# A first MLP whose weight sums are made in device memory during the attention, with two plain groups instead of three

## The chip, the cores and the metric

The kernel runs on one core of a Trainium2 chip. A core has a matrix engine (TensorE, "PE" in the profile), a vector engine (VectorE, "DVE"), an activation engine (ScalarE, "ACT"), a general engine (GpSimd, "POOL"), and a queue engine (SyncE, "SP") that issues loads. Sixteen DMA engines move data between device memory and the core's on-chip memory (SBUF). Plain loads are issued by SP and form queue 1 (hardware_dynamic); a DMA that adds to its destination is issued by POOL and forms queue 0 (software_dynamic). Each engine runs its instructions in order, and waits on semaphores where an operand or a buffer is not ready. TensorE accumulates into eight banks of PSUM. The metric is the device time of the whole program in microseconds (us).

## The reference, cut to what matters

The program is a two-layer decoder trunk on 512 tokens of width 1024, all in float32. Layer 0 is attention and an MLP, layer 1 a gated short convolution and an MLP.

```python
h = x
h = h + attention_mixer(h, ...)       # 8 softmax heads, 8 stick-breaking heads, one output projection
h = h + conv_ffn(h, ...)              # the "first MLP"
h = h + short_conv_mixer(h, ...)
h = h + conv_ffn(h, ...)

def conv_ffn(h, norm_g, w_up, conv_w, w_down):      # D_FF = 2816
    xn = rms_norm(h, norm_g)
    u = causal_dwconv(xn @ w_up, conv_w)            # w_up: 1024 x 5632
    g, val = u[..., :D_FF], u[..., D_FF:]
    return (jax.nn.silu(g) * val) @ w_down
```

The change concerns `xn @ w_up` of the first MLP.

## The kernel before

**Precision.** Every float32 operand of a product is split into a high and a low half (ScalarE copies the high half, VectorE subtracts it to give the low one), and each product is three matmuls: high x high, high x low, low x high. So each weight tile of 128 x 1024 costs a DMA, one ScalarE copy (`whi`) and one VectorE subtraction (`wlo`).

**Plain weights.** `want` lists weight tiles in the order of use; `weights()` hands out the next and at once emits the load and split of the tile two further on (`fetch`, `load`, `split_all`; SP issues at L256, the splits are L262 and L263). Loaded tiles live in a ring of three buffers with the tag `raw`, the halves in rings of three `whi` and three `wlo`. SP runs ahead of the other engines: a load is issued as soon as the split three tiles before it has freed a `raw` buffer. The attention's query and key weights are loaded as 128 columns at a time, rows of 512 bytes, 1024 rows a tile; its value weights as 256 columns, 512 rows of 1024 bytes.

**The attention.** Twenty-four units (head pair by query blocks) run in a software pipeline: `logits` of unit g, then `weigh` of an earlier one and `turn` (transposes) of unit g-1, with projections as fillers between (`fill`). ScalarE takes exponentials and sigmoids out of the score banks and copies the high halves out of the transposes; it also does the weight splits, in the same queue. POOL does little there: some constants, a memset of `fwide` (L494), and small memsets of the `rest` tile in the stick-breaking heads (L687, L690).

**The first MLP's up projection.** The output columns are handled in 11 groups of 256 gate and 256 value columns (`HF` = 11). A *plain* group (0, 1 and 2; `CLASSIC = 3`) is four blocks of 128 columns; each block is 8 x 3 matmuls of 512 columns into one bank (`products`, L283 to L285). The other groups, *seven groups*, use a block scheme with seven products in place of eight (`Sevens`): the tokens are split in two halves of 256, the 1024 inputs in two halves of 512, and the columns into gate and value. Each product (`seven`, L1011) is 24 matmuls of 256 columns. Products are called p1, p7, p3, p6, p2, q5, q4, one per *slot*, and each has a weight operand and a token operand (a "form", made once by `prepare` from the normalised residual). With X, Y, W, Z for the four 512 x 256 weight blocks (first inputs gate, first inputs value, last inputs gate, last inputs value), the weight operands are: p1: X; p2: W; p3: Z; p7: Y + Z; p6: Y + Z + X; q4: Y + Z + X + W; q5: X + Y. Before, Y is loaded by SP, the Z block is added by an accumulating DMA from POOL (`add_block`), and VectorE then adds X (L1063) and W (L1111) in place; Y is added onto X by another accumulating DMA.

**Order.** The program is written to a planner that orders each engine's instructions by its own estimate of readiness. An instruction wrapped in `pin` (or `keep_in_program_order`) stays behind what was written before it on its engine; this sets an order and no wait for any other engine. Work of VectorE and ScalarE that is not urgent (normalising plain groups' outputs, preparing forms, the convolution and gate of plain groups) is written as generators in a list of *chores*, each step with a nominal cost; `work_off(us)` runs that much of it. It is called per matmul triple in plain blocks with `SHARE` = 0.58, and per slot in the first seven group.

**Banks.** Tags a, b and c have 2, 4 and 2 of the eight banks. A plain block's accumulator is freed when its `normed` chore has read it.

**The convolution stage** uses the same class `Sevens` with `ahead = True`; its p6 weights are split in slot 1, after a copy of the first product's bank to another bank (L1102) on ScalarE.

Of the kernel before, what the change touches and what calls it, by code (L numbers as in the profile page):

```python
# [25 lines left out]
P = 128  # L26
S = 512
# [26 lines left out]
def trunk(  # L54
# [384 lines left out]
    def want_conv_out():  # L439
        for o in range(ND):  # L440
            want(conv_w_out[0], 0, 8, o * P, P)
        want_ffn(1, 2 * CLASSIC)

    want_ffn(0, 2 * CLASSIC)

    def products(acc, w, order=tuple(range(ND))):
        for k in order:
# [188 lines left out]
    def logits(p, u):  # L636
# [33 lines left out]
        if fox:  # L670
            m = len(bs)
            top, total, inv = (tiny.tile([P, m, 2], F32, tag=f"{t}{m}", name=f"{t}{p}{u}") for t in ("top", "total", "inv"))
            for j, (b, n, c, a) in enumerate(parts):
                for e in range(2):
                    dve.reduce_max(top[:, j, e:e + 1], ss[e][:, c:c + n], axis=AX.X, negate=True)
                    act.activation(own[j][:, e, :], ss[e][:, c:c + n], AF.Exp, bias=top[:, j, e:e + 1], accum_out=total[:, j, e:e + 1])
            for es in at_once(u):
                dve.reciprocal(inv[:, :, es], total[:, :, es])
                for j in range(m):
                    for e in range(es.start, es.stop):  # L680
                        dve.tensor_scalar(own[j][:, e, :], own[j][:, e, :], inv[:, j, e:e + 1], None, op0=ALU.mult)
        else:

            scale = q_scale[p]
            if not rests:
                rests.append(aw.tile([P, 2, S + 1], F32, tag="rest", name="rest", bufs=1))
                pool.memset(rests[0][:, :, S:S + 1], 0.0)  # L687
# [328 lines left out]
    class Sevens:  # L1016

        def __init__(self, name, mp, groups, block_of):
            self.name, self.mp, self.groups, self.block_of = name, mp, groups, block_of
            self.forms = {n: [mp.tile([P, 4, HT], F32R, tag=f"{n}_{i}", name=f"{n}_{i}{name}") for i in ("hi", "lo")] for n in FORMS}  # L1020
            self.st, self.wides = {}, {}
# [7 lines left out]
        def load_one(self, g, n, kh, half):  # L1029
            t = self.st[g][n] = wp.tile([P, CHUNK], F32, tag="raw", name=f"{n}{self.name}{g}")[:, 0:1024].rearrange("p (k c) -> p k c", c=2 * P)  # L1030
            nc.sync.dma_start(t, self.block_of(g, kh, half))
# [28 lines left out]

        def first_sums(self, g):
            self.weights_of(g, "p7", "Y")
            dve.tensor_tensor(self.st[g]["Y"], self.st[g]["Y"], self.st[g]["X"], op=ALU.add)  # L1063
# [11 lines left out]
        def slot(self, g, s):  # L1075

            on, was, soon = (i in self.groups for i in (g, g - 1, g + 1))
            if g == self.groups[0]:
                self.work_off(1.4 if s < 4 else 1e9)
            form, n, fresh = (("p1", "A", True), ("p7", "T", True), ("p3", "R", False), ("p6", "R", False), ("p2", "A", False),  # L1080
                              ("q5", "R", False), ("q4", "T", False))[s]
            if s == 2:
# [5 lines left out]
            if s == 0:  # L1088
# [2 lines left out]
                        self.weights_of(p, "p3", "Z")  # L1091
                    self.join(p, "yg", st[p]["T"], st[p]["Xs"])
                if on:
                    self.load_one(g, "W", 1, 0)
                if soon:
                    self.load_pair(g + 1)
            elif s == 1:
                first = not was and not self.ahead
                if on and first:
                    self.weights_of(g, "p6", "Y")  # L1100
                if on:
                    act.activation(self.bank_of(g, "R"), c["A"], AF.Copy, scale=-1.0)  # L1102
                if on and not first:
                    self.weights_of(g, "p6", "Y")
                if soon:
                    self.add_block(g + 1, "Y", 1, 1)
            elif s == 2:
                if on:
                    self.kept(g, "P7s", c["T"])
                    self.weights_of(g, "p2", "W")  # L1110
                    dve.tensor_tensor(c["Y"], c["Y"], c["W"], op=ALU.add)  # L1111
            elif s == 3:
                if was:
                    self.early(p, st[p]["R"])
                if on:
                    self.weights_of(g, "q5", "X")
            elif s == 4:
                if on:
                    self.kept(g, "Xs", c["R"])
                    self.weights_of(g, "q4", "Y")  # L1120
            if was and s != 2:
                self.tail(p, s)
            if s == 5:
                if on:
                    self.load_one(g, "Z", 1, 1)
                    self.open_wides(g)
                    self.left(g, c["A"])
                if soon:
# [7 lines left out]
                    self.first_sums(g + 1)  # L1136

        chores, credit, ahead = (), 0.0, False

        def work_off(self, us):  # L1140
            if self.norm.row is None:
# [9 lines left out]
    def up_seven(layer, norm, mp):  # L1151

        blocks = Blocks(mp, layer)
        w_up, base = ffn_w_up[layer], CLASSIC
# [5 lines left out]
        up = Sevens(layer, mp, range(CLASSIC, HF), block_of)  # L1160
        up.norm, up.chores = norm, []
        up.wides_of = lambda g: {n: mp.tile([P, 2, S], F32, tag=n, name=f"{n}{layer}{g}", bufs=1) for n in ("yg", "yv", "ug", "uv")}
        wides, forms, chores = up.wides, up.forms, up.chores

        def taps_of(g, half, i):
# [49 lines left out]
            blocks.product(2 * g + i, 1, u[0][:, i:i + 1, :], u[1][:, i:i + 1, :])  # L1215
            yield 0.86

        for j in range(2 * CLASSIC):
            accs = []
            for half in range(2):  # L1220
                accs.append(bank("ab"[half]))
                for _ in products(accs[-1], weights()):
                    up.work_off(SHARE)
                if j == 2 * CLASSIC - 1 and half == 1:
                    up.weights_of(base, "p1", "X")
                    up.first_sums(base)
            if j == 2 * CLASSIC - 2:
                up.load_pair(base)
                up.add_block(base, "Y", 1, 1)
# [5 lines left out]
        slots = [(lambda g=g, s=s: up.slot(g, s)) for g in range(CLASSIC, HF + 1) for s in range(7)]  # L1235
        return blocks, slots

    def conv_seven(norm, mp):
# [109 lines left out]
        for j in range(8):  # L1348
# [26 lines left out]
    def mlp(layer, norm, mp):  # L1375
# [60 lines left out]
                else:  # L1436
                    pin(dve.tensor_tensor(b, b, d, op=ALU.add))

        n_up = 7 * (HF - CLASSIC)
        for i, fn in enumerate(slots[:n_up]):  # L1440
            fn()
            left = n_up - i
# [177 lines left out]
```

## Time and profile before

| what | value |
|---|---|
| median of 3 runs | 1133.82 us (1133.34 to 1135.28) |
| profiled execution | 1133.66 us |
| its span, first to last instruction | 1131.9 us |
| TensorE busy | 1120.0 us, 99% |
| VectorE busy | 965.3 us, 85% |
| ScalarE busy | 670.5 us, 59% |
| queue 1 (plain loads) | 106.94 MB, 30.7% of 16 DMA engines |
| queue 0 (issued by POOL) | 47.10 MB, 25.0% |

In the profile a group of instructions is named by its line, its engine, its operation and its tiles (`out<-in`). "Busy" of TensorE counts pipelined matmuls whose ends are modelled. In a timeline the first column is the start and the second the duration in us, and the brackets hold how long the engine was idle before, and what ended that. A DMA view gives for each queue its packets, megabytes and the time its packets took as a share of sixteen engines over the stretch. By time, the attention runs from about 40 to 275 us, the first MLP's up projection from 280 to 513 us (plain groups until 347 us), its down projection to about 620 us, the convolution stage from there to about 760 us, and then comes the second MLP.

### The profile page before, as it was taken

Reading aid. Unit: us, or ns where it says so; the run is one execution under the profiler, and the core shown is the slowest. Engines: PE = TensorE matmul, PEld = TensorE weight load, DVE = VectorE, ACT = ScalarE, POOL = GpSimd, SP = SyncE. Lnnn points to the kernel's source line nnn. Section 1 sums busy time; section 2 is a strip of 40 time slices with the busy share of each in tenths; the row PEclk is TensorE's granted clock in tenths of the full one; section 3 lists DMA queues with packets and bytes.
Section 4 is the critical chain, followed back from the end, with each engine's and each line's share of the span. In section 5 each row is a group of like instructions: output and inputs, shape, how many; then the busy total and the mean of one; then the engine's idle time right before and its main releaser. Section 6 shows DMA issues by size and latency. Waiting matters only on the chain.

```text
span 1131.9 us, 19049 instructions
## 1 busy us (share of the span) xinstructions
PE 1120.0 (99%) x7547; PEld 1005.0 (89%) x7547; DVE 965.3 (85%) x1459; ACT 670.5 (59%) x999; POOL 133.0 (12%) x150
## 2 busy tenths in 40 slices
PE   8999999999999999999999999999999999999998
PEld 6888787878889999999999889988889999998886
DVE  5787888887899899989989889875798899989886
ACT  7556676655455766666557455543445767667554
POOL 4000000000002111014400001000002111014300
PEclk9999999999999999999999999999999999999999
DMA  6412212032375877789963455533375876789961
GB/s 193 113 38 75 57 38 75 21 93 75 94 195 113 182 176 152 178 222 216 227 179 77 115 152 132 124 112 93 94 195 112 176 184 146 177 224 220 228 160 56
DMA packets 160440, 155.31 MB, mean 137 GB/s; under 512 B 6396, under 2 KB 136492, under 8 KB 160352
## 3 DMA queue, kind: packets, MB, share of 16 engines
q1 hardware_dynamic: 124256, 106.94, 30.7%
q0 software_dynamic: 35936, 47.10, 25.0%
q8 instruction: 59, 0.97, 0.4%
q14 instruction: 29, 0.24, 0.1%
q10 hardware_dynamic: 160, 0.07, 0.0%
HBM read 149.10 MB, written 2.10 MB: 134 GB/s over the span
## 4 chain that ended last, share of the span: by engine, by line
PE 90%; DVE 5%; ACT 2%; DMA 1%; issue 1%; SPq 0%; DVEq 0%; ACTq 0%
PE psb L1011 24%; PE psb L1532 11%; PE psa L1011 10%; PE psa L1532 8%; PE psb L283 6%; PE psb L285 6%; PE psb L284 6%; PE psa L285 4%; PE psa L284 4%; PE psa L283 4%; PE psb L658 1%; PE psa L754 1%; DVE rest L699 1%; DVE wlo L263 1%; DMA X<-in_ffn_w_up 1%; PE psc L730 1%
## 5 line engine op out<-in xcount | busy, mean ns | idle before, releaser
L262 ACT ACTIVATE whi<-raw 128x1024 fp32r<-128x1024 f32 (+2 forms) x97 | 100.1, 1033 | 97.3 <-PE psa L284 29.2
L263 DVE TENSOR_TENSOR wlo<-raw,whi 128x1024 fp32r<-128x1024 f32 (+2 forms) x97 | 115.3, 1190 | 26.0 <-ACT whi L262 25.1
L1011 PE MATMUL psb<-p_lo,whi_p 128*128 128x256 f32 x384 | 108.1, 281 | 0.0
L1011 PE MATMUL psb<-p_hi,wlo_p 128*128 128x256 f32 x384 | 108.1, 281 | 0.0
L1011 PE MATMUL psb<-p_hi,whi_p 128*128 128x256 f32 x384 | 107.8, 281 | 0.0
L283 PE MATMUL psb<-hs_a,whi 128*128 128x512 f32 x256 | 104.8, 409 | 0.0
L285 PE MATMUL psb<-hs_a,wlo 128*128 128x512 f32 x256 | 101.4, 397 | 0.0
L1011 PEld LDWEIGHTS psb<-p_hi,whi_p 128*128 128x128 f32 x384 | 72.8, 190 | 0.0
L1011 PEld LDWEIGHTS psb<-p_lo,whi_p 128*128 128x128 f32 x384 | 72.3, 188 | 0.0
L1011 PE MATMUL psb<-q_hi,whi_q 128*128 128x256 f32 x256 | 72.1, 282 | 0.2 <-ACT Xs L1059 0.2
L1011 PE MATMUL psa<-p_hi,wlo_p 128*128 128x256 f32 x256 | 72.2, 282 | 0.0
L1011 PEld LDWEIGHTS psb<-p_hi,wlo_p 128*128 128x128 f32 x384 | 72.2, 188 | 0.0
L1011 PE MATMUL psb<-q_hi,wlo_q 128*128 128x256 f32 x256 | 72.1, 282 | 0.0
L1011 PE MATMUL psb<-q_lo,whi_q 128*128 128x256 f32 x256 | 72.0, 281 | 0.0
L1011 PE MATMUL psa<-p_lo,whi_p 128*128 128x256 f32 x256 | 72.0, 281 | 0.0
L1011 PE MATMUL psa<-p_hi,whi_p 128*128 128x256 f32 x256 | 71.8, 281 | 0.0
L1532 PE MATMUL psb<-act,whi 128*128 128x256 f32 x352 | 63.0, 282 | 0.1
L393 DVE SCALAR_TENSOR_TENSOR uv<-yv,taps,uv 128x511 f32<-128x511 f32 (+1 forms) x88 | 62.9, 745 | 0.2
L393 DVE SCALAR_TENSOR_TENSOR ug<-yg,taps,ug 128x511 f32<-128x511 f32 (+1 forms) x88 | 62.1, 745 | 0.3 <-ACT ug L390 0.3
L285 PEld LDWEIGHTS psb<-hs_a,wlo 128*128 128x128 f32 x256 | 48.1, 188 | 11.2 <-DVE wlo L263 0.2
L283 PEld LDWEIGHTS psb<-hs_a,whi 128*128 128x128 f32 x256 | 48.4, 189 | 10.5 <-issue 1.2
L1532 PE MATMUL psb<-whi,act 128*128 128x512 f32 x176 | 56.5, 398 | 0.0
(458 smaller groups left out, 3643.4 us busy)
## 6 DMA issues: line engine op xcount, KB each, us to landing
raw<-in_attn_w_in SPq DMA_DIRECT2D x24, 512.0 KB, 3.9
raw<-in_ffn_w_up SPq DMA_DIRECT2D x24, 512.0 KB, 3.8
X<-in_ffn_w_up SPq DMA_DIRECT2D x16, 512.0 KB, 4.7
W<-in_ffn_w_up SPq DMA_DIRECT2D x16, 512.0 KB, 6.8
Y<-in_ffn_w_up SPq DMA_DIRECT2D x16, 512.0 KB, 4.4
Z<-in_ffn_w_up SPq DMA_DIRECT2D x16, 512.0 KB, 4.7
Y<-in_ffn_w_up POOLq DMA_DIRECT2D x16, 512.0 KB, 9.8
X<-in_ffn_w_up POOLq DMA_DIRECT2D x16, 512.0 KB, 7.5
```

Of the source, the lines that this page charges most:

```text
L262: return (act.activation(hi[:, at_], raw[:, at_], AF.Copy), dve.tensor_tensor(lo[:, at_], raw[:, at_], f32(hi[:, at_]), op=ALU.subtract))
L263: dve.tensor_tensor(lo[:, at_], raw[:, at_], f32(hi[:, at_]), op=ALU.subtract))
L283: made = [pe.matmul(acc, w[0], rhs[0], start=first, stop=False), pe.matmul(acc, w[0], rhs[1], start=False, stop=False), pe.matmul(acc, w[1 ...
L284: pe.matmul(acc, w[0], rhs[1], start=False, stop=False),
L285: pe.matmul(acc, w[1], rhs[0], start=False, stop=last)]
L393: dve.scalar_tensor_tensor(dst[:, d:], src[:, 0:S - d], tap(j), dst[:, d:], op0=ALU.mult, op1=ALU.add)
L658: pe.matmul(ss[e][:, c:c + wide], ql[rows, b * P:n], kl[rows, 0:wide], start=first and b == bs[0], stop=last and b == bs[-1])
L699: dve.tensor_tensor_scan(back, back, begin[:, S - n:S][:, ::-1], 0.0, op0=ALU.mult, op1=ALU.max)
L730: pe.transpose(t[:, k * P:(k + 1) * P], w[:, e, k * P:(k + 1) * P], ident)
L754: pe.matmul(out_, w, t[:, first:first + step * (NB - k - 1) + 1:step, :], start=k == 0 and i == 0, stop=k == NB - 1 and i == 1)
L1011: pe.matmul(to, w[a][:, k, c], x[b][:, k, :], start=fresh and i + k + t == 0, stop=i == 1 and k == 3 and t == 2, skip_group_check=not fresh)
L1532: pe.matmul(to, l, r, start=begin and o + t == 0, stop=end and t == 2 and o == (0 if layer else 1), skip_group_check=not fresh)
```

## The change

Five things change: three belong to the first MLP, one to the attention, one to the convolution stage.

1. `PLAIN = 2, 3`: in the first MLP two plain groups, in the second still three. The plain blocks' banks become a, b / a, b / b, b / c, c. In the loop over plain blocks only group 0 is normalised and both halves of the forms prepared; group 0's gates and all of group 1 become chores that are worked off during the seven groups, 1.4 us a slot in the first and 0.5 us a slot after it. Group 1's wide tiles live in the space of `hs_a`.
2. `table_steps` makes three tables in device memory, for groups 2 to 10 in three chunks of three groups: "7" = Y + Z, "6" = that plus X, "4" = that plus W. It takes six steps of three DMAs, all on POOL's queue, each 512 rows of 768 floats: a copy, an accumulate, a copy of the made table, an accumulate, and again. They are handed out one by one, one before the attention's `fill(PRE)` and one per unit, each pinned behind POOL's last instruction.
3. In the first MLP's seven groups the sums are loaded as plain blocks: Y comes from table 7, two further loads bring "p6 sum" and "q4 sum" into the `raw` ring, and both VectorE additions and Y's accumulating DMA go. SP's loads of these groups are pinned. X's accumulating DMA stays.
4. The memsets of the stick-breaking `rest` tile move from POOL to VectorE.
5. In the convolution stage the p6 weights of its first group are split before the slots rather than in slot 1.

```diff
-CLASSIC = 3
+PLAIN = 2, 3
+CHUNKS = (2, 3), (5, 3), (8, 3)
...
+    far = ctx.enter_context(tc.tile_pool(name="far", bufs=1, space=bass.MemoryType.DRAM))
...
+    tables = {}
+
+    def table_steps():
+
+        w = ffn_w_up[0]
+        for n in "764":
+            for g, m in CHUNKS:
+                tables[n, g] = far.tile([512, m * 256 + 16], F32, tag=f"t{n}{g}", name=f"t{n}{g}")
+        def block(kh, half, g, m):
+            return w[kh * 512:(kh + 1) * 512, half * DFF + g * 256:half * DFF + (g + m) * 256]
+        for step in range(6):
+            n = "764"[step // 2]
+            for g, m in CHUNKS:
+                to = tables[n, g][:, 0:m * 256]
+                if step % 2:
+                    src = block(*((0, 1), (0, 0), (1, 0))[step // 2], g, m)
+                    pin(nc.gpsimd.dma_start(to, src, accum_op=ALU.add))
+                else:
+                    pin(nc.gpsimd.dma_start(to, block(1, 1, g, m) if step == 0 else tables["76"[step // 2 - 1], g][:, 0:m * 256]))
+                yield
+
+    def table_of(n, group):
+        g, m = next(c for c in CHUNKS if c[0] <= group < c[0] + c[1])
+        return tables[n, g][:, (group - g) * 256:(group - g + 1) * 256].rearrange("(k p) c -> p k c", p=P)
...
-                pool.memset(rests[0][:, :, S:S + 1], 0.0)
+                dve.memset(rests[0][:, :, S:S + 1], 0.0)
             rest = rests[0]
             if u == 0:
-                pool.memset(rest[:, :, P:P + 1], 0.0)
+                dve.memset(rest[:, :, P:P + 1], 0.0)
...
+    sums_far = table_steps()
+    next(sums_far)
     fill(PRE)
     for g in range(len(units) + 2):
+        next(sums_far, None)
...
-            nc.sync.dma_start(s["X"], self.block_of(g, 0, 0))
-            nc.sync.dma_start(s["Y"], self.block_of(g, 0, 1))
+            self.held(nc.sync.dma_start(s["X"], self.block_of(g, 0, 0)))
+            self.held(nc.sync.dma_start(s["Y"], self.table("7", g) if self.table else self.block_of(g, 0, 1)))
...
         def first_sums(self, g):
             self.weights_of(g, "p7", "Y")
-            dve.tensor_tensor(self.st[g]["Y"], self.st[g]["Y"], self.st[g]["X"], op=ALU.add)
+            if not self.table:
+                dve.tensor_tensor(self.st[g]["Y"], self.st[g]["Y"], self.st[g]["X"], op=ALU.add)
             self.add_block(g, "X", 0, 1)
+            if self.table:
+                self.load_one(g, "p6 sum", self.table("6", g))
...
-            if g == self.groups[0]:
-                self.work_off(1.4 if s < 4 else 1e9)
+            if self.chores:
+                self.work_off(self.rate(g, s))
...
-                first = not was and not self.ahead
-                if on and first:
-                    self.weights_of(g, "p6", "Y")
+                first = not was
+                if on and first and not self.ahead:
+                    self.weights_of(g, "p6", "p6 sum" if self.table else "Y")
...
-                if soon:
+                if soon and not self.table:
                     self.add_block(g + 1, "Y", 1, 1)
...
-                    dve.tensor_tensor(c["Y"], c["Y"], c["W"], op=ALU.add)
+                    if self.table:
+                        self.load_one(g, "q4 sum", self.table("4", g))
+                    else:
+                        dve.tensor_tensor(c["Y"], c["Y"], c["W"], op=ALU.add)
...
+        if layer == 0:
+            up.table = table_of
+            up.rate = lambda g, s: 1.4 if g == base else 0.5
...
+                accs.append(bank(("ab", "ab", "bb", "cc")[j][half] if layer == 0 else "ab"[half]))
...
+            if layer == 0:
+                if j < 2:
+                    chores.extend((normed(0, j, accs), prepare(j)))
+                continue
...
+        if layer == 0:
+            chores.extend([gate_one(0, i) for i in range(2)] + [normed(1, i, kept[2 + i]) for i in range(2)] + [gate_one(1, i) for i in range(2)])
...
                 up.first_sums(1)
+                up.weights_of(1, "p6", "Y")
         want_conv_out()
```

More of the change, by code (lines that the diff above doesn't have):

```diff
@@ L1020, in __init__ @@
             self.forms = {n: [mp.tile([P, 4, HT], F32R, tag=f"{n}_{i}", name=f"{n}_{i}{name}") for i in ("hi", "lo")] for n in FORMS}
-            self.st, self.wides = {}, {}
+            self.st, self.wides, self.table = {}, {}, None
         def load_pair(self, g):
@@ L1025, in load_pair, with held, load_one @@
             s["X"], s["Y"] = (self.mp.tile([P, 4, 2 * P], F32, tag=t, name=f"{t}{self.name}{g}", bufs=2) for t in "XY")
-            nc.sync.dma_start(s["X"], self.block_of(g, 0, 0))
-            nc.sync.dma_start(s["Y"], self.block_of(g, 0, 1))
-        def load_one(self, g, n, kh, half):
+            self.held(nc.sync.dma_start(s["X"], self.block_of(g, 0, 0)))
+            self.held(nc.sync.dma_start(s["Y"], self.table("7", g) if self.table else self.block_of(g, 0, 1)))
+        def held(self, made):
+            if self.table:
+                pin(made)
+        def load_one(self, g, n, src):
             t = self.st[g][n] = wp.tile([P, CHUNK], F32, tag="raw", name=f"{n}{self.name}{g}")[:, 0:1024].rearrange("p (k c) -> p k c", c=2 * P)
-            nc.sync.dma_start(t, self.block_of(g, kh, half))
+            self.held(nc.sync.dma_start(t, src))
         def add_block(self, g, n, kh, half):
@@ L1103, in slot @@
                 if on and not first:
-                    self.weights_of(g, "p6", "Y")
-                if soon:
+                    self.weights_of(g, "p6", "p6 sum" if self.table else "Y")
+                if soon and not self.table:
                     self.add_block(g + 1, "Y", 1, 1)
@@ L1119, in slot @@
                     self.kept(g, "Xs", c["R"])
-                    self.weights_of(g, "q4", "Y")
+                    self.weights_of(g, "q4", "q4 sum" if self.table else "Y")
             if was and s != 2:
@@ L1138, in trunk, with rate @@
         chores, credit, ahead = (), 0.0, False
+        def rate(self, g, s):
+            return 1.4 if s < 4 else 1e9
         def work_off(self, us):
@@ L1158, in block_of, with wides_of @@
             return w_up[kh * 512:(kh + 1) * 512, c0:c0 + 2 * P].rearrange("(k p) c -> p k c", p=P)
-        up = Sevens(layer, mp, range(CLASSIC, HF), block_of)
+        up = Sevens(layer, mp, range(base, HF), block_of)
         up.norm, up.chores = norm, []
-        up.wides_of = lambda g: {n: mp.tile([P, 2, S], F32, tag=n, name=f"{n}{layer}{g}", bufs=1) for n in ("yg", "yv", "ug", "uv")}
+        if layer == 0:
+            up.table = table_of
+            up.rate = lambda g, s: 1.4 if g == base else 0.5
+        def wides_of(g):
+            if layer == 0 and g == base - 1:
+                t = hsp.tile([P, 8, S], F32, tag="hs_a", name=f"hs_a_wide{layer}")
+                return {n: t[:, 2 * i:2 * i + 2, :] for i, n in enumerate(("yg", "yv", "ug", "uv"))}
+            return {n: mp.tile([P, 2, S], F32, tag=n, name=f"{n}{layer}{g}", bufs=1) for n in ("yg", "yv", "ug", "uv")}
+        up.wides_of = wides_of
         wides, forms, chores = up.wides, up.forms, up.chores
@@ L1216, in gate_one @@
             yield 0.86
-        for j in range(2 * CLASSIC):
+        kept = []
+        for j in range(2 * base):
             accs = []
             for half in range(2):
-                accs.append(bank("ab"[half]))
+                accs.append(bank(("ab", "ab", "bb", "cc")[j][half] if layer == 0 else "ab"[half]))
                 for _ in products(accs[-1], weights()):
                     up.work_off(SHARE)
-                if j == 2 * CLASSIC - 1 and half == 1:
+                if j == 2 * base - 1 and half == 1:
                     up.weights_of(base, "p1", "X")
                     up.first_sums(base)
-            if j == 2 * CLASSIC - 2:
+            if j == 2 * base - 2:
                 up.load_pair(base)
-                up.add_block(base, "Y", 1, 1)
+                if not up.table:
+                    up.add_block(base, "Y", 1, 1)
+            kept.append(accs)
+            if layer == 0:
+                if j < 2:
+                    chores.extend((normed(0, j, accs), prepare(j)))
+                continue
             chores.append(normed(j // 2, j % 2, accs))
@@ L1234, in up_seven @@
                 chores.append(gate_one(i // 2, i % 2))
-        slots = [(lambda g=g, s=s: up.slot(g, s)) for g in range(CLASSIC, HF + 1) for s in range(7)]
+        if layer == 0:
+            chores.extend([gate_one(0, i) for i in range(2)] + [normed(1, i, kept[2 + i]) for i in range(2)] + [gate_one(1, i) for i in range(2)])
+        slots = [(lambda g=g, s=s: up.slot(g, s)) for g in range(base, HF + 1) for s in range(7)]
         return blocks, slots
```

13 lines of the change are left out of this document (7 added, 6 removed).

## The prediction

> **What bounds the kernel now.** I read the page first, then the busy times by stretch, then the waits by engine, and last the DMA queues and the order of the loads in the attention. From the page come the span, the engines, and TensorE, granted clock and DMA in 40 slices of 28.3 us:
>
> ```profile
> span 1131.9 us, 19049 instructions
> PE 1120.0 (99%) x7547; PEld 1005.0 (89%) x7547; DVE 965.3 (85%) x1459; ACT 670.5 (59%) x999; POOL 133.0 (12%) x150
> PE   8999999999999999999999999999999999999998
> PEclk9999999999999999999999999999999999999999
> DMA  6412212032375877789963455533375876789961
> ```
>
> TensorE is busy 1120.0 of 1131.9 us at full clock: time is won by giving it less to do, and lost wherever it is made to wait. The DMA engines are mostly idle in slices 3 to 11 (the attention) and busy in the MLP. The profiled execution took 1133.66 us, 1.8 us around its span and 0.16 under the median 1133.82; I sum against 1133.7.
>
> The next rows are two stretches: the last plain group of the first MLP, four blocks of 24 matmuls, then one group of seven products (the columns are length, busy time and count of PE, PEld, DVE, ACT, POOL, then clock, DMA share and GB/s).
>
> ```profile
> 324.61:346.97 22.36, 22.36 (x98) 18.06 (x96) 21.59 (x34) 10.76 (x16) 2.49 (x2) 1.00 0.61 156
> 367.52:387.41 19.89, 19.89 (x171) 19.89 (x170) 18.32 (x24) 13.36 (x17) 4.23 (x5) 1.00 0.77 172
> ```
>
> Neither has idle TensorE. A plain group costs 22.36 us, a seven group 19.89. All that TensorE waited between 346 and 500 us is one row, and in the convolution stage one more:
>
> ```profile
> PE psb L1011 <- ACT Xs L1059: 0.2, 1, 0.2
> PE psb L1011 <- DVE wlo_p6c L961: 0.9, 1, 0.9
> ```
>
> **The change, part by part.** *One plain group becomes a seven group:* 22.36 - 19.89 = 2.47 us less of TensorE, all of it on the path. The entry from plain blocks into the first seven group is the same code one group earlier.
>
> *Fewer sums on VectorE and POOL.* Per group two additions and one accumulating DMA go. The groups view of 360 to 480 us has the additions:
>
> ```profile
> L1111 DVE TENSOR_TENSOR Y<-Y,W 128x1024 f32<-128x1024 f32 x6 | 7.4, 1226 | 0.2
> L1063 DVE TENSOR_TENSOR Y<-Y,X 128x1024 f32<-128x1024 f32 x6 | 7.3, 1224 | 0.2
> ```
>
> That is 2.45 us a group, some 22 us over nine groups. TensorE does not wait for VectorE there, so it is worth nothing by itself; it pays for chores. VectorE is busy 18.32 of 19.89 us, so 1.57 + 2.45 = 4.0 us are free, and the moved chores ask 7 x 0.5 = 3.5 by their rate. Tight, for two groups: between 0 and 1 us of waits, I take 0.2.
>
> *Preparing the forms in less time.* They need both halves done before the first seven product, now at 324.61. VectorE gets the norm's row at 294.26:
>
> ```profile
> 294.26 0.69 DVE L1206 TENSOR_TENSOR yg<-psa,nrow_n 128x512 f32<-128x512 f32 x1 [1.08 <-ACT nrow_n L344]
> 295.46 1.41 DVE L1190 SCALAR_TENSOR_TENSOR X_prep<-h,gains,nrow_n 128x512 f32<-128x512 f32 x2
> 298.11 1.22 DVE L263 TENSOR_TENSOR wlo<-raw,whi 128x1024 fp32r<-128x1024 f32 x1
> 299.85 0.69 DVE L1197 TENSOR_TENSOR Y_prep<-X_prep 128x512 f32<-128x512 f32 x1
> ```
>
> Each half is 4 x 0.71 + 11 x 0.69 = 10.4 us, the four products by the row 2.8, four remaining plain splits and one of the group 5 x 1.22 = 6.1: 29.7 in the 30.35 us there are. It fits; it has no cover beyond 0.6 us, and the gates come after it.
>
> *More loads in a group.* One accumulate goes, two plain 512 KB loads come (the sums of p6 and q4). The tightest is q4's: its buffer is free when the previous group's Z is split, near the start of the group, and it is wanted some 10 us later, against this landing:
>
> ```profile
> Z<-in_ffn_w_up SPq DMA_DIRECT2D x16, 512.0 KB, 4.7
> ```
>
> I cost it at nothing; without that margin each late microsecond of a load is one of TensorE, once a group. The SP queue is now pinned, so a load that waits for its buffer holds those behind it; all come a half group ahead.
>
> *The convolution stage.* Its p6 split is moved ahead of the slots. The stall now, by the three engines' timelines:
>
> ```profile
> 664.23 1.22 DVE L1063 TENSOR_TENSOR Yc<-Yc,Xc 128x1024 f32<-128x1024 f32 x1
> 666.47 0.58 ACT L1102 ACTIVATE psb<-psa 128x512 f32<-128x512 f32 x1 [7.37 <-PE psa L1011]
> 670.47 0.39 PE L1011 MATMUL psb<-p_hic,wlo_p6c 128*128 128x256 f32 x1 [0.94 <-DVE wlo_p6c L961]
> 671.59 1.22 DVE L961 TENSOR_TENSOR wlo_p2c<-Wc,whi_p2c 128x1024 fp32r<-128x1024 f32 x1
> ```
>
> ScalarE idles 7.37 us and could split p6 once the sum is made at 665.45; 1.06 + 1.22 us later (a weight split on either engine, rows below and above), at 667.7, both halves stand, before TensorE wants them at 669.53. Late next is p2, ready at 672.81 and wanted a product (19.89 / 7 = 2.84 us) after 669.53, at 672.37. So 0.5 to 0.94 us are won; I take 0.8.
>
> *Five memsets move from POOL to VectorE*, 0.10 us each: 0 to 0.5 us lost, I take 0.2. The gain is 2.47 + 0.8 - 0.2 - 0.2 = 2.9 us.
>
> *The eighteen table transfers.* Each moves 512 rows of 3072 B, nine as copies and nine as accumulates, on POOL's queue 0. What paces them? They are handed out one per unit of the attention, but that is only their order on POOL, pinned behind what POOL did before. POOL's own work then:
>
> ```profile
> 40.80 0.53 POOL L494 MEMSET fwide<- 128x512 f32 x1 [19.27 <-PE psc L610]
> 143.21 0.10 POOL L687 MEMSET rest<- 128x2 f32 x1 [101.87 <-PE psb L658]
> ```
>
> The second row and its followers leave POOL. So nothing holds the tables after 41.3 us but their own landings, and with three chunks in rotation one is always moving: they run in one burst. Its length comes from DMA views of four stretches: an accumulate of 2048 B rows alone (524 to 528), copies of 4096 B on queue 0 (541 to 543), accumulates of 1024 B beside 512 B loads (728 to 730), and 2048 B beside 2048 B (549 to 559):
>
> ```profile
> q0 software_dynamic: 424, 0.82, 113.0%
> ...
> q0 software_dynamic: 135, 0.48, 70.6%
> ...
> q0 software_dynamic: 268, 0.27, 83.4%
> q1 hardware_dynamic: 287, 0.15, 35.8%
> ...
> q0 software_dynamic: 668, 1.27, 68.9%
> q1 hardware_dynamic: 681, 1.33, 40.1%
> ```
>
> Accumulates move 0.82 MB in 4 us, 205 GB/s: a 3072 B record takes one of 16 engines 3072 x 16 / 205e3 = 0.24 us. Copies moved 0.48 MB in 2 us, 0.20 us a record; by their share of the engines (70.6% of 32 engine-us over 135 packets, 0.167 us for about 4096 B) 0.125. I take 0.16 between them; device memory as a destination isn't in this trace, so the upper bound of a copy is the accumulate's 0.24, and of an accumulate, with that same step on top, 0.30. A transfer has 32 records per engine, so the burst is 9 x 32 x (0.16 + 0.24) = 115 us, with the loads beside it about 130: from 42 to 172 us.
>
> The last two pairs matter most: with both queues full, the packets go one for one, 268 to 287 and 668 to 681, whatever their sizes. A weight load of the attention is 1024 packets of 512 B, 64 per engine. Alone it lands in 3.8 us:
>
> ```profile
> raw<-in_attn_w_in SPq DMA_DIRECT2D x1, 512.0 KB, 3.8
> q1 hardware_dynamic: 12880, 7.70, 21.7%
> ```
>
> (The second row is 42 to 172 us: 805 load packets per engine, beside which the tables have 18 x 32 = 576.) In turns with table records it takes 64 x (0.16 + 0.03) = 12 us beside copies, 64 x (0.24 + 0.03) = 17 beside accumulates; 0.03 is 21.7% x 130 x 16 / 12880. Issue and use of loads now, from the SP and ScalarE timelines:
>
> ```profile
> 62.81 0.37 SPq L256 DMA_DIRECT2D raw<-in_attn_w_in  x1
> 69.98 0.37 SPq L256 DMA_DIRECT2D raw<-in_attn_w_in  x1
> 90.44 0.37 SPq L256 DMA_DIRECT2D raw<-in_attn_w_in  x1
> 90.20 1.06 ACT L262 ACTIVATE whi<-raw 128x1024 fp32r<-128x1024 f32 x1
> 96.47 1.06 ACT L262 ACTIVATE whi<-raw 128x1024 fp32r<-128x1024 f32 x1 [0.67 <-PE psb L284]
> 104.47 1.06 ACT L262 ACTIVATE whi<-raw 128x1024 fp32r<-128x1024 f32 x1 [1.74 <-issue]
> 115.27 1.06 ACT L262 ACTIVATE whi<-raw 128x1024 fp32r<-128x1024 f32 x1 [1.02 <-PE psb L284]
> ```
>
> The fourth row's split uses the load of the first, and so on; each load is issued as the split three before it frees its buffer. Tables alternate: copies 42 to 59 us, accumulates to 85, copies to 103, accumulates to 128, copies to 147, accumulates to 172. Loads are served in order: that of 62.81 waits for its forerunners, which I reckon served by 78, and lands near 92 (2 late for 90.20); that of 69.98 near 104 (8 late), of 90.44 near 121.5 (17 late), the next near 136 against 115.27 (20 late). The values' loads have half the packets, so it stays at 13 to 18 late and is made up after 172. The split stands in ScalarE's order, and behind it the softmax, the evacuations and the transposes' halves; TensorE, with four score banks, runs dry some time after. How long it can go on, one row bounds from below, a ScalarE wait without a gap on TensorE:
>
> ```profile
> 134.66 0.58 ACT L676 ACTIVATE w<-psb,top 128x384 f32<-128x384 f32 x1 [3.63 <-DVE top L675]
> ```
>
> From above, one interval of splits, (115.27 - 90.20) / 3 = 8.4 us. I take 5 us of cover. TensorE loses 20 - 5 = 15 us. With the low copy price (0.125) the largest lateness is 13 and the loss 8; with 0.24 for copies it is 31; with 0.30 for accumulates too, some 43.
>
> The Trainium skill, "DMA: Bandwidth & Descriptors", section "Queues, rings and completion order", says that an engine changes queues only after a whole packet, typically 9 to 17 descriptors. By that rule a load would need 4 to 7 turns, not 64, and would land 1 to 2 us later than alone: no loss, the time of the first rival below. The two pairs above count one for one, against the rule as far as they go.
>
> The same page, "Latency and other measured facts", has copies within device memory at 207 to 214 GB/s, an estimated 0.23 us a record here; by that the sum would be near 1160. No run here shows it.
>
> Sum: 1133.7 - 2.9 + 15 = 1145.8 us.
>
> **Rivals.** *The loads pass the tables.* If the engine lets several small load records through per table record, or the planner puts the splits where a late load hurts nobody, the loss is 0 and the time 1133.7 - 2.9 = 1130.8. For it: every load here lands long before its split, 20 us and more. Against it: the two pairs. It decides where the 64 turns of a load fit into the 8.4 us between two splits: 0.13 us a turn, where I reckon 0.19 and 0.27.
>
> *Device memory is dear.* Reading and writing there costs 0.24 for copies and 0.30 for accumulates: the burst lasts past 200 us, and 1133.7 - 2.9 + 31 to 43 = 1162 to 1174.
>
> *The forms come late.* Loads pass, but the 0.6 us left on VectorE before 324.61 is not enough, and TensorE waits 1 to 3 us for the first seven product or the third; then 1132 to 1134, no change.
>
> **How the numbers follow.** Loads held at the middle prices 0.45, at the dear ones 0.20, loads pass 0.28, forms late 0.07. The measurement tells 0.2% or 2.3 us from no change. So faster 0.28, same 0.07, slower 0.65. The range takes in the loads that pass (1130.8, and 1 us under it) and most of the dear case: 1129.5 to 1170; the forecast's own is 1138 to 1162.
>
> **What would show it.** Right: queue 0 full from about 42 us in one stretch of 115 us or more; in it landings of the attention's loads of 10 to 20 us; TensorE idle behind ScalarE's weight splits between 90 and 170, 10 us and more in all; the stages after shifted by that, less one group of 22.36 against 19.89; no 0.94 us wait at the convolution's p6. Wrong: landings under 8 us beside a full queue 0, or late loads with TensorE at 10 of 10 in every stretch; or tables spread over the whole attention.

## The result, and the profile after

The changed kernel takes 1179.6 us in the median of five runs (1176.49 to 1180.35) against 1133.82: the ratio is 1.0393, 95% interval 1.0376 to 1.0411, so about 45 us were lost. The forecast was 1145.8 with a range of 1129.5 to 1170. The direction and the place were as forecast; the size was not.

The page of the changed kernel, which answers to the page shown before:

```profile
span 1177.6 us, 19211 instructions
PE 1132.7 (96%) x7619; PEld 1018.4 (86%) x7619; DVE 949.4 (81%) x1447; ACT 676.1 (57%) x1006; POOL 138.8 (12%) x156
PE   8987479999999999999999999999999999999998
PEclk9988689999999999999999999999999999999999
DMA  6799981212235787769994327543356786779961
...
t<-in_ffn_w_up POOLq DMA_DIRECT2D x12, 1536.0 KB, 20.4
raw<-in_attn_w_in SPq DMA_DIRECT2D x24, 512.0 KB, 5.8
...
t<-t POOLq DMA_DIRECT2D x6, 1536.0 KB, 19.1
```

Slices of 29.4 us now. TensorE was at 9 of 10 through the attention, and is at 7, 4 and 7 in slices 4 to 6; the DMA row has 7, 9, 9, 9, 8 in slices 2 to 6, where it had 4, 1, 2, 2, 1. From slice 7 on TensorE's rows look the same in both kernels. The issue list has the twelve plus six table transfers, each about 20 us from issue to landing.

Where the time was lost shows in the starts of two matmuls on TensorE's timeline: the first of the first MLP's plain blocks (`psb<-hs_a`) and the first seven product (`psa<-p_hi`). The first two rows are of the kernel before, the other two of the changed kernel, in whose numbering L283 has become L311 and L1011 L1042.

```profile
278.86 0.39 PE L283 MATMUL psb<-hs_a,whi 128*128 128x512 f32 x1
...
347.20 0.28 PE L1011 MATMUL psa<-p_hi,whi_p 128*128 128x256 f32 x1
```

```profile
326.13 0.39 PE L311 MATMUL psb<-hs_a,whi 128*128 128x512 f32 x1
...
372.11 0.28 PE L1042 MATMUL psa<-p_hi,whi_p 128*128 128x256 f32 x1
```

The attention ends 326.13 - 278.86 = 47.27 us later. The first seven product, at 347.20 before, is 24.91 us late, and the difference, 22.36 us, is exactly the plain group that is gone. Both kernels then run seven groups at 19.89 us, so with the extra group the down projection begins 44.8 us late, and it stays at 45 to the end. The loss lies in the attention, whole.

The next rows are the groups of waits of the changed kernel between 40 and 300 us (total, times, longest), and ScalarE's timeline at the last four of the five weight splits that wait for a load there (L290 was L262):

```profile
ACT whi L290 <- DMA raw<-in_attn_w_in: 51.0, 5, 12.9
DVE wlo L291 <- ACT whi L290: 49.2, 8, 12.5
PE psc L605 <- ACT sq L648: 9.1, 1, 9.1
```

```profile
107.47 1.06 ACT L290 ACTIVATE whi<-raw 128x1024 fp32r<-128x1024 f32 x1 [11.66 <-DMA raw<-in_attn_w_in]
124.53 1.06 ACT L290 ACTIVATE whi<-raw 128x1024 fp32r<-128x1024 f32 x1 [12.29 <-DMA raw<-in_attn_w_in]
142.93 1.06 ACT L290 ACTIVATE whi<-raw 128x1024 fp32r<-128x1024 f32 x1 [12.90 <-DMA raw<-in_attn_w_in]
161.31 1.06 ACT L290 ACTIVATE whi<-raw 128x1024 fp32r<-128x1024 f32 x1 [8.88 <-DMA raw<-in_attn_w_in]
```

ScalarE now waits 51 us at five splits, VectorE as long behind it, and TensorE then behind what ScalarE has not done (9.1 us at a squares' copy, for one). The four splits stood at 90.20, 96.47, 104.47 and 115.27 before. They are now 17 to 18 us apart, one load each. The first is 17.3 us late and the last 46.0, which is the loss of the attention but for 1.2 us.

Why a load takes 17 us: DMA views of the changed kernel, 64 to 76 us (accumulates) and then 130 to 136 us (copies); packets, MB and share of the engines by queue.

```profile
q0 software_dynamic: 735, 2.19, 93.8%
q1 hardware_dynamic: 729, 0.37, 15.3%
...
q0 software_dynamic: 325, 1.87, 92.4%
q1 hardware_dynamic: 327, 0.17, 10.6%
```

In both, the queues advance packet for packet, 735 to 729 and 325 to 327. A pair, one packet of each queue, occupies one of the 16 engines for 16 x the stretch / the pairs. Beside accumulates a pair takes 12 x 16 / 732 = 0.26 us. Beside copies it takes 6 x 16 / 326 = 0.29, since a packet of a copy holds two rows: 1.87 MB in 325 packets is some 5.8 KB each, where the accumulates' 2.19 MB in 735 packets is one row of 3 KB.

Equal counts alone would also come out if each queue sent several packets at a turn. The packets' own times in the trace tell the two apart. Between 130 and 136 us a table packet starts within 4 ns of the end of a load's packet 354 times, and a load's packet within 4 ns of the end of a table packet 346 times; neighbouring steps of 4 ns hold 45 to 95 such pairs, which is chance among 16 engines. Between two packets of the same queue there is no such peak (42 and 72). So the turns are single packets.

### The profile page after: what moved, and what is told of

It is laid out like the page before. It is cut to its first block, busy times and chain, and to the rows that moved or that the text cites. A ratio compares the mean times of both kernels' runs of the same rounds, so it can differ in the third digit from the quotient of the medians.

```text
span 1177.6 us, 19211 instructions
## 1 busy us (share of the span) xinstructions
PE 1132.7 (96%) x7619; PEld 1018.4 (86%) x7619; DVE 949.4 (81%) x1447; ACT 676.1 (57%) x1006; POOL 138.8 (12%) x156
## 4 chain that ended last, share of the span: by engine, by line
PE 82%; DMA 8%; DVE 4%; issue 2%; ACT 2%; another core or an unknown queue 1%; SPq 0%; DVEq 0%; ACTq 0%; POOLq 0%
PE psb L1042 23%; PE psb L1595 10%; PE psa L1042 9%; PE psa L1595 8%; DMA raw<-in_attn_w_in 7%; PE psb L311 5%; PE psb L313 4%; PE psb L312 4%; PE psa L311 3%; PE psa L313 3%; PE psa L312 3%; PE psa L782 2%; DMA Xc<-in_conv_w_in 1%; PE psb L686 1%; DVE wlo L291 1%
## 5 line engine op out<-in xcount | busy, mean ns | idle before, releaser
L290 ACT ACTIVATE whi<-raw 128x1024 fp32r<-128x1024 f32 (+2 forms) x93 | 95.9, 1033 | 140.4 <-DMA raw<-in_attn_w_in 51.0
L291 DVE TENSOR_TENSOR wlo<-raw,whi 128x1024 fp32r<-128x1024 f32 (+2 forms) x93 | 110.5, 1189 | 70.1 <-ACT whi L290 69.3
L1042 PE MATMUL psb<-p_lo,whi_p 128*128 128x256 f32 x408 | 115.0, 282 | 0.0
L1042 PE MATMUL psb<-p_hi,wlo_p 128*128 128x256 f32 x408 | 114.9, 282 | 0.0
L1042 PE MATMUL psb<-p_hi,whi_p 128*128 128x256 f32 x408 | 114.8, 281 | 0.0
L311 PE MATMUL psb<-hs_a,whi 128*128 128x512 f32 x240 | 101.1, 421 | 6.0 <-ACT qk L656 6.0
L1042 PEld LDWEIGHTS psb<-p_hi,whi_p 128*128 128x128 f32 x408 | 77.3, 190 | 0.0
L1042 PEld LDWEIGHTS psb<-p_lo,whi_p 128*128 128x128 f32 x408 | 76.9, 189 | 0.0
L1042 PE MATMUL psa<-p_hi,wlo_p 128*128 128x256 f32 x272 | 76.8, 282 | 0.0
L1042 PE MATMUL psa<-p_lo,whi_p 128*128 128x256 f32 x272 | 76.7, 282 | 0.0
L1042 PE MATMUL psb<-q_lo,whi_q 128*128 128x256 f32 x272 | 76.6, 282 | 0.0
L1042 PEld LDWEIGHTS psb<-p_hi,wlo_p 128*128 128x128 f32 x408 | 76.6, 188 | 0.0
L1042 PE MATMUL psb<-q_hi,wlo_q 128*128 128x256 f32 x272 | 76.6, 281 | 0.0
L1042 PE MATMUL psb<-q_hi,whi_q 128*128 128x256 f32 x272 | 76.5, 281 | 0.0
L1042 PE MATMUL psa<-p_hi,whi_p 128*128 128x256 f32 x272 | 76.5, 281 | 0.0
L1069 POOL DMA_DIRECT2D X<-in_ffn_w_up x17 | 22.3, 1313 | 375.3 <-DVE wlo_p L992 274.2
L311 PEld LDWEIGHTS psb<-hs_a,whi 128*128 128x128 f32 x240 | 46.8, 195 | 16.3 <-ACT qk L656 6.4
```

The lines of the kernel that those rows point to most:

```text
L290: return (act.activation(hi[:, at_], raw[:, at_], AF.Copy), dve.tensor_tensor(lo[:, at_], raw[:, at_], f32(hi[:, at_]), op=ALU.subtract))
L291: dve.tensor_tensor(lo[:, at_], raw[:, at_], f32(hi[:, at_]), op=ALU.subtract))
L311: made = [pe.matmul(acc, w[0], rhs[0], start=first, stop=False), pe.matmul(acc, w[0], rhs[1], start=False, stop=False), pe.matmul(acc, w[1 ...
L1042: pe.matmul(to, w[a][:, k, c], x[b][:, k, :], start=fresh and i + k + t == 0, stop=i == 1 and k == 3 and t == 2, skip_group_check=not fresh)
```

## The experiments

**1. Is the loss the tables' at all?** The changed kernel without them, and the old kernel with them.

```diff
 # e1_no_tables, on the changed kernel
-            up.table = table_of
+            up.table = lambda n, group: block_of(group, *{"7": (0, 1), "6": (1, 1), "4": (1, 0)}[n])
...
-    sums_far = table_steps()
-    next(sums_far)
+    sums_far = iter(())
```

> The changed kernel without the eighteen table transfers; its seven groups load single weight blocks in place of the sums, the same sizes and rows from the weights themselves, so the three sums of each group (p7, p6, q4) are left out and the output is not the reference's. Theory (the tables' records hold the attention's loads): all of the loss goes, and the gain that the prediction summed stays: 1133.7 - 2.9 = 1130.8 us, between 1130 and 1132. Rival (the extra loads, the moved chores or the planner's new order cost the time): it stays above 1150.

```diff
 # e2_tables_alone, on the kernel before; nothing loads from the tables
...
+    sums_far = table_steps()
+    next(sums_far)
     fill(PRE)
     for g in range(len(units) + 2):
+        next(sums_far, None)
```

> The kernel before with the eighteen table transfers added at the same place and unused (and the small memsets on VectorE). Theory: the whole loss appears, 47 us by the stages' starts, so 1178 to 1183. Rival (the loss needs the changed up projection): 1134 to 1140.

Measured: without tables 1130.85 us (ratio to before 0.9976, 0.9966 to 0.9986), tables alone 1181.16 (1.0416, 1.0402 to 1.0431). So the tables alone cost 47.2 us and the other edits together gain 3.1. The two give a loss of 44.2 us, against 45.8 measured. The rival that the new up projection costs something falls.

**2. Turns or bytes?** If a load's packet waits for one packet of queue 0, then shorter packets, longer load packets, or fewer load packets beside the burst must all help, with the bytes unchanged.

```diff
 # e3_rows_1k: 54 transfers of 1024 B rows
-CHUNKS = (2, 3), (5, 3), (8, 3)
+CHUNKS = tuple((g, 1) for g in range(2, 11))
...
-        next(sums_far, None)
+        for _ in range(3):
+            next(sums_far, None)
```

> The changed kernel with nine chunks of one group in place of three of three: the same bytes in 54 transfers with rows of 1024 B, three handed out per unit. Theory (a load's record waits for one record of queue 0, whatever its size): an accumulate's record falls from 0.24 to 0.083 us, a copy's from about 0.28 to 0.10, so a load of 64 turns lands after 7 to 9 us in place of 17 to 20; the loads come every 8.4 us, so they end at most 2 us late, and the time is 1131 to 1135. Rival (queue 0 takes the bandwidth, by bytes): 1170 and more, since bytes and burst are the same.

```diff
 # e6_loads_1k: tables as in the change; query and key loads as 512 rows of 1024 B
+            pairs = list(zip(parts[::2], parts[1::2]))
+            if dram is w_in and pairs[0][1] == P:
+                c0 = pairs[0][0] // 256 * 256
+                v, nk_, pairs = raw[:, 0:nk * n].rearrange("p (k c) -> p k c", c=256), 4, [(c0, 256)]
...
```

> The changed kernel, tables untouched, with the attention's query and key weight loads taken as 512 rows of 1024 B in place of 1024 rows of 512 B: the same bytes into the same tiles, but other columns, so the projections are not the reference's. Theory of turns: a load has 32 turns of 0.27 to 0.31 us, 9 to 10 us in place of 17 to 20, which fits between two splits: the loss falls to 0 to 4 us, the time is 1130 to 1135. Rival by bytes or by memory bandwidth: no change, 1176 to 1181.

```diff
 # e4_late: all tables behind the first memset of `rest`, which stays on POOL
-                dve.memset(rests[0][:, :, S:S + 1], 0.0)
+                pool.memset(rests[0][:, :, S:S + 1], 0.0)
+                run(sums_far)
...
-    next(sums_far)
...
-        next(sums_far, None)
```

> The changed kernel with all table transfers behind the first small memset of the stick-breaking part, left on POOL, which POOL got at 143 us before: the burst runs from about 143 to 275 us. Theory of turns: the loads there are of 512 and 256 records (32 and 16 turns, 9 and 5 us), every 10 us or so, only three or four of 1024 stand at its start and some at its end; TensorE loses 0 to 10 us: 1131 to 1142. Rival by bytes: the same burst beside the same megabytes per us of loads, so nearly the same loss, 1160 and more.

Measured: rows of 1 KB 1133.15 us (0.9992, 0.9983 to 1.0001); loads in 1 KB packets 1130.5 (0.9978, 0.9966 to 0.9990); late 1139.75 (1.0061, 1.0042 to 1.0080). All three fall where turns put them, and 20 to 46 us below the lowest time that bytes would give (1160 for the late tables, 1170 and 1176 for the other two). The views of one stretch each, 60 to 70 us of the kernel with 1 KB table rows and then 64 to 76 us of that with 1 KB loads:

```profile
q0 software_dynamic: 1369, 1.42, 84.9%
q1 hardware_dynamic: 1371, 0.69, 34.3%
```

```profile
q0 software_dynamic: 678, 2.03, 86.9%
q1 hardware_dynamic: 680, 0.68, 20.9%
```

Again one for one. In the first a pair takes 10 x 16 / 1370 = 0.117 us, 64 of them 7.5 us. That stretch holds accumulates. The copies of this kernel didn't shrink as expected: the trace has them in packets of 4096 B, four rows each, and between 94 and 100 us 535 packets of queue 0 go beside 537 of the loads, 0.18 us a pair. A load takes some 11 us there, where 7 to 9 was expected; the copies are the smaller part of the burst. In the second a pair is 0.28, but a load has 32. That the DMA engines are as full as in the changed kernel, and TensorE hardly waits, shows in one stretch of each, 42 to 196 and 42 to 172 us, and then in the kernel before, 42 to 172 us (length; busy of PE, PEld, DVE, ACT, POOL; clock; DMA share; GB/s):

```profile
42.00:196.00 154.00, 152.19 (x1042) 123.99 (x1040) 127.02 (x309) 99.58 (x213) 44.30 (x52) 1.00 1.08 242
```

```profile
42.00:172.00 130.00, 129.44 (x907) 107.08 (x906) 107.39 (x266) 82.18 (x179) 13.62 (x16) 1.00 1.05 270
```

```profile
42.00:172.00 130.00, 129.44 (x907) 107.08 (x906) 107.45 (x265) 82.81 (x180) 0.14 (x2) 1.00 0.22 60
```

The second has TensorE's 129.44 us of the kernel before, beside a DMA share of 1.05 and 270 GB/s. In the changed kernel the same stretch has a DMA share of 1.05 and 257 GB/s too, and TensorE is busy 95.96 us: full engines by themselves don't hold TensorE up.

**3. Copies or accumulates?** The term that I had sized wrong was the copies' turn. Does it carry the loss?

```diff
 # e8_accum_1k: accumulates cut into 256 columns; e9_copy_1k does the same to the copies alone
-                    pin(nc.gpsimd.dma_start(to, src, accum_op=ALU.add))
+                    for i in range(m):
+                        c = slice(i * 256, (i + 1) * 256)
+                        pin(nc.gpsimd.dma_start(to[:, c], src[:, c], accum_op=ALU.add))
```

> The changed kernel with only the accumulates cut into transfers of one group (rows of 1024 B, turns of 0.11 us beside a load), the copies left as they are (records of 6144 B, turns of 0.31 us). Reckoned load by load as in the prediction, but with these measured turns: loads land 20 us after they begin in a copy step and 7 in an accumulate step, which come in alternation, so the lateness never builds up: 1131 to 1136 us. If the copies' long records carry the loss by themselves, it stays above 1150.

> The changed kernel with only the copies cut into transfers of one group (records of 4096 B, turns of 0.23 us), the accumulates left at rows of 3072 B (turns of 0.27 us). By the same reckoning with measured turns the largest lateness is 30 us and TensorE loses 24 to 30: 1155 to 1161 us. If the copies' records carry the loss, it falls to 1140 or below.

Measured: accumulates cut 1137.33 us (1.0033, 1.0019 to 1.0046), copies cut 1157.87 (two runs; 1.0216, 1.0186 to 1.0245). The second is in its range, the first 1.3 us above its own. The waits for loads, with the accumulates cut and then with the copies cut:

```profile
ACT whi L292 <- DMA raw<-in_attn_w_in: 9.3, 1, 9.3
```

```profile
ACT whi L293 <- DMA raw<-in_attn_w_in: 30.1, 4, 11.2
```

The waits follow the loss. Against the kernel without tables, 1130.85 us, the changed kernel loses 48.8 us and ScalarE's splits wait 51.0 us for loads; with the copies cut it is 27.0 and 30.1, with the accumulates cut 6.5 and 9.3. The answer to the question is no: with the copies left long, 6.5 us are lost. Cutting the copies wins 22 us, cutting the accumulates 42, more together than there is to win. The two cuts are not alike, though: in their traces the copies' packets shrink from 6144 to 4096 B, the accumulates' from 3072 to 1024, so the runs don't rank the two kinds. That the lateness goes once the mean turn brings loads as fast as they are used fits both times, but was reckoned and not measured.

**4. The convolution stage's edit alone.**

```diff
 # e5_conv_only, on the kernel before
-                first = not was and not self.ahead
-                if on and first:
+                first = not was
+                if on and first and not self.ahead:
...
                 up.first_sums(1)
+                up.weights_of(1, "p6", "Y")
```

> The kernel before with the convolution stage's p6 split moved ahead of the slots, alone. The prediction's term: 0.5 to 0.94 us won, 0.8 taken: ratio 0.9993. Rival (the wait only moves to the next product of that stage, as the copy Xs showed a wait of 0.5 to 0.7 us in the runs with the move): 0 to 0.5 us lost, ratio 1.0000 to 1.0004.

Measured: 0.9994 (0.9986 to 1.0003). The forecast's 0.9993 and no effect both lie within. In its trace TensorE's wait at p6 is gone and none takes its place, but in the changed kernel a new one of 0.5 us stands in that stage, and in the kernel without tables (e1) this one of 0.7:

```profile
PE psb L1041 <- ACT Xsc L1093: 0.7, 1, 0.7
```

So the wait goes when the edit stands alone and comes back in part together with the rest; what it is worth in time is not shown.

**5. A version that beats both.** Rows of 1 KB and the tables behind POOL's first memset of `rest`:

```diff
 # e7_late_rows_1k = e3's first edit and e4's
-CHUNKS = (2, 3), (5, 3), (8, 3)
+CHUNKS = tuple((g, 1) for g in range(2, 11))
```

> Both remedies: the tables in rows of 1024 B and all behind the first small memset at 143 us. Theory of turns: the loads there have 32 or 16 turns of about 0.13 us, so they land 4 us later than alone and nothing waits; what is left is the gain of the kernel without tables, 1130.9, between 1130 and 1132.5. If the burst costs something beside the loads (ScalarE, POOL, memory), it stays at 1133 or above as with the rows alone.

Measured: 1131.62 us, 0.9981 (0.9971 to 0.9990) of the kernel before. That is 2.2 us faster, within its expected range, and 0.8 us over the kernel that has no tables to make, a difference the intervals don't separate.

## Why the prediction was right or wrong

*The gain, 2.9 us:* right as a sum. The kernel without tables measured 1130.85 us, where the forecast's rival "the loads pass the tables" had 1130.8; the interval of its ratio allows 1.6 to 3.9 us of gain. The group exchange shows to the hundredth (22.36 against 19.89 us). For late forms, tight chores and extra loads there is no wait of TensorE between the first seven product and the down projection in the list of waits, so they stayed as small as assumed. The convolution's 0.8 us was partly given back (experiment 4).

*What paces the tables:* right. The first transfer leaves POOL at 40.51 us, right behind the memset, and queue 0 is full until about 168 us; I had 42 to 172.

*One packet for one, whatever their sizes:* right, in the stretches in which both queues stayed full. The Trainium skill, "DMA: Bandwidth & Descriptors", section "Queues, rings and completion order", has an engine drain a whole packet of 9 to 17 descriptors before it changes queues; no stretch here shows that ratio. The prediction got "no loss" from that rule by taking such packets for the loads alone: with as many table rows in a turn of queue 0, a load would wait as long as in single turns. So its equal counts were not yet an argument against the rule; the order of the packets between 130 and 136 us is.

*The failed step:* "In turns with table records it takes 64 x (0.16 + 0.03) = 12 us beside copies". I had taken the price of a copied row from packets of 4096 B on queue 0 and divided it by bytes, when their very size said how the queue packs copies: those loads had rows of 2048 B. A copy's packet holds two rows. The bytes' price was fine (the burst's length came out), but what a load waits for is the packet, so its turn beside copies is 0.29 us, not 0.19, and a load takes 64 x 0.29 = 19 us there, more than the 17 beside accumulates. There is then no step in which loads catch up. The prediction's own reckoning with 0.29 in place of 0.19 has the four loads land near 102, 120, 138 and 155 us, an estimate, so the fourth split is 40 us late where I had 20. They were issued at 62.09, 73.80, 95.93 and 109.81 us and landed 45.4, 50.7, 46.9 and 51.4 us later, at 107.5, 124.5, 142.8 and 161.2, each behind those before it. The 4 to 6 us by which each is later still are not turns. The load ahead of them, issued at 46.05 us, sent its first packet only at 50.56; why is not shown. With these microseconds the fourth split is the measured 46 us late. The sign that I had named, landings of 10 to 20 us, holds for the distance between two landings (17 to 19 us), not from issue to landing.

*A second step:* "I take 5 us of cover". The attention ended 47.3 us late and the split 46.0, so no cover is left to see. I had read a single wait without a gap as room in the pipeline. That a lateness which comes back at every load uses such room up once is an explanation that no run tests.

*The clock* was in no term. In five stretches of the attention the granted clock fell to half, all shown whole here:

```profile
72.50:79.30 6.80, 5.18 (x41) 3.95 (x42) 4.04 (x8) 3.92 (x12) 0.64 (x1) 0.50 1.09 213
106.60:116.80 10.20, 5.46 (x26) 4.46 (x27) 4.47 (x9) 3.26 (x7) 0.92 (x1) 0.50 1.09 213
123.70:133.90 10.20, 6.90 (x20) 4.88 (x21) 4.78 (x12) 4.93 (x13) 0.65 (x2) 0.50 1.05 347
137.30:150.90 13.60, 6.38 (x26) 5.17 (x27) 6.03 (x15) 5.94 (x12) 2.03 (x2) 0.50 1.05 240
164.60:171.40 6.80, 4.45 (x15) 3.77 (x16) 5.11 (x11) 3.14 (x8) 0.00 (x0) 0.50 1.01 263
```

TensorE is busy 28.36 us in them, so at most 14 us of its time are due to the clock. While loads set the pace this is hidden, as TensorE waits anyway. The loads set it at least until 161.31 us, where the last late split, 46.0 us behind, had still waited 8.88 us for its load. Only 1.2 of the 47.3 us came after that, so the clock can't be much of the loss; a run without its falls was not made.

*The dear device memory:* the rival's 1162 to 1174 was nearer in size, but its reason did not hold. An accumulate cost 0.26 us a turn with the load's 0.03 in it, as the accumulates into SBUF had it, not 0.30, and copies moved at about 1.87 MB in 6 us, faster than I had taken.

## What to carry to other kernels

A transfer "in the idle time of the DMA engines" is not free when it is made of long packets. In the stretches shown here each packet of a load that shared an engine with it waited for one of them. So count the load's packets per engine, multiply by the other queue's packet time, and compare that with the interval at which the loads are used. The remedies tried here cost nothing in bytes: shorter rows for the background, longer ones for the loads that somebody waits for, or another moment, held there by an instruction that really waits. Take the packet's size from the trace's counts, not from the row in the code.

## What the runs showed of the hardware that was not expected

- Copies on the software queue pack rows, accumulates don't: in the tables 1.87 MB went in 325 packets as copies, and 2.19 MB in 735 as accumulates, of the same 3072 B rows.
- The DMA engines did a copy and an accumulate within device memory at no worse a price than one into SBUF. By the queues' own time, an accumulate of 3 KB took 93.8% of 12 x 16 us over 735 packets, 0.245 us, and one of 2 KB into SBUF 0.171 (113.0% of 4 x 16 over 424). Copies moved 1.87 MB in 6 us, 312 GB/s, beside loads.
- While loads queue up, issuing one takes longer too. An SP instruction that issues a load of the attention takes 0.37 us in the median of both kernels; the longest is 3.1 us before and 12.0 us in the changed kernel. One of the long ones:

```profile
73.80 10.85 SPq L284 DMA_DIRECT2D raw<-in_attn_w_in  x1
```

- TensorE's clock fell to half inside idle stretches of 3.33, 7.72, 5.95, 9.07 and 7.01 us in the changed kernel's attention, and stayed there for 6.8, 10.2 or 13.6 us, as in the rows above, part of it with TensorE still idle. The Trainium skill, "TensorE: Matmul & The Clock Gate", Part 1, gives a window of about 3.4 us for it; two, three and four windows fit these lengths.
